# Spreading the sample states over more ticks and reordering a norm's pilot, extra columns and row tokens

## The chip, the cores and the metric

One NeuronCore of a Trainium2 chip runs the whole program. The metric is the device time of one execution in microseconds (us); of several runs the median is given. The engines are named as in the profile: PE (TensorE, matmuls), DVE (VectorE), ACT (ScalarE), POOL (GpSimd) and SP (SyncE, which here only issues DMAs). Each engine works through its instructions in the order written; where one waits, all behind it on that engine wait too.

## The reference

One layer of a hybrid decoder is computed for 256 prompt tokens and 8 sample tokens (T = 264 columns), width 2048, in float32:

- `proj = x @ w_in`, cut into z, x/B/C, dt, the short convolution's three parts and two gates;
- A: a Mamba-2 SSD mixer (32 heads of 64, 4 groups, state 128) with a causal convolution before it. For the prompt it is a chunked scan. Each of the 8 samples takes one step on a state of its own: `h = h * exp(dt*A) + (x*dt) B`, `y = h C`; the new states (8 x 2048 x 128) are outputs;
- B: a gated short convolution; `mix = sigmoid(g_a) * (yA @ w_branch_ssd) + sigmoid(g_b) * (yB @ w_branch_sc)`;
- `x1 = LN(ALPHA*x + mix @ w_out)`, then `x2 = LN(ALPHA*x1 + PEER(x1))`, where PEER picks 16 of 16384 single-neuron experts for each of 8 heads, and last `y = x2 + sigmoid(x2 @ ple_gate_w) * (p @ ple_proj_w)`.

## The kernel before

**Weights and matmuls.** Activations lie transposed: 128 rows of the width by the tokens. Weights come in 1 MB tiles `w` (16 blocks of 128 x 128) that SP fetches in a written-out order (`fetch`, L146) into a ring of three. `split_w` cuts each half tile in two: `whi`, a rounded copy made by ACT (L158), and `wlo`, the remainder made by DVE (L159), into four pairs of buffers, later five. `col_block` computes 128 output rows in two halves, each of 8 x 3 matmuls (L255 whi by x high, L256 whi by x low, L257 wlo by x high). `pair_block` does the same for the experts' matrices with two matmuls a block (L293, L294, L296).

**Ticks.** After each half block `tick` is called. It first runs what `defer` and `soon` have put by for this tick, then lets the background tasks, which are Python generators, go on in the order of their list. A number that a task yields is taken from the tick's credit (0.9 to 1.3, an estimate of VectorE's time), and `("w", n)` lets the task rest for n ticks. All of this is fixed when the program is built: it sets only the order of the instructions on each engine. `soon` is the next tick, or the one after it where it is called from an evacuation.

**Sample states.** `ssd_samples` goes over 64 units of 256 state rows. An iteration issues, for units of different age: the store of the new state (POOL, L659), the read-out `jk` (two on DVE, L665), the update (two on DVE, L675), the scaling by the decay (two on ACT, L681), and the loads of a state tile `h0t` (SP, L692; a ring of eight) and of B and C (SP, L696; every second unit). It runs beside the x/B/C blocks (24 column blocks, with a convolution evacuated by `conv_evac`), the short convolution's blocks (48, `sc_c`, `sc_h`, `sc_b`), and `ssd_group`, the prompt's scan (four groups; ACT loads `arow`, L557). SP's queue holds the weight fetches and the state loads in one order. Ahead of the z stage `run_out` gives ticks with no matmul until scan and samples are done.

**Norms.** `Norm` takes 16 blocks as they are evacuated (`add`). The first block gives a pilot mean (`pilot`: PE L876, ACT L878), which is subtracted from all (`gather`, DVE L886). For each block j the scaled block is written as a high part `h` (ACT, L894) and a low part `l` (DVE, L910), squares are taken (ACT, L895), sums kept (DVE, L912 or L915), and two extra columns of gain and bias are put into `h` and `l` (POOL, L896, L897); the next matmul reads all of it. In the second norm the 208 prompt columns come from the V product (`v_evac`: L1480, L1482), and the other 56 columns, the row tokens, whose experts are gathered row by row on POOL, come later from `rest`: for each j a high part (ACT, L948), a copy (POOL, L949) and a low part (DVE, L952). The PLE product (`ple_half`, L1559 to L1561) comes behind the last block of V, then the norm's statistics, then the last 16 column blocks.

Of the kernel before, what the change touches and what calls it, by code (L numbers as in the profile page):

```python
# [20 lines left out]
T = PT + NS  # L21
# [30 lines left out]
def hybrid_step(ctx: ExitStack, tc: tile.TileContext, xT, pT, w_in, w_dt, w_bs, w_bc, w_o, w_q, w_pg, w_pp,  # L52
# [590 lines left out]
    def ssd_samples():  # L643

        while len(XS) < 4 or "dexp" not in S or "bc" not in S:
            yield ("w", 1)
        dexp = S["dexp"]
        xds, hts, bcs = {}, {}, {}
        units = [(g, s, a) for g in range(GRP) for s in range(NS) for a in range(2)]
        n = len(units)  # L650

        def rows(t, u):
            g, s, a = units[u]
            return t[s, 512 * g + 256 * a:512 * g + 256 * a + 256, :].rearrange("(q p) n -> p q n", p=128)

        u = 0
        while u < n + 4:
            if 0 <= u - 4:
                gp.dma_start(out=rows(o_hs, u - 4), in_=hts.pop(u - 4))  # L659
            if 0 <= u - 3 < n:  # L660
                v = u - 3
                g, s, a = units[v]
                for q in range(2):
                    jk = ab("jk", width=128)
                    ve.scalar_tensor_tensor(jk, hts[v][:, q], 1.0, bcs[v // 2][:, 1], OP.mult, OP.mult,  # L665
                                            accum_out=ysum[:, 4 * g + 2 * a + q, s:s + 1])
                if (s, a) == (NS - 1, 1):
                    for q in range(4):
                        j = 4 * g + q
                        ve.scalar_tensor_tensor(XS[j][:, PT:], XS[j][:, PT:], col(P_D, j), ysum[:, j], OP.mult, OP.add)  # L670
            if 0 <= u - 2 < n:
                v = u - 2
                g, s, a = units[v]
                for q in range(2):
                    ve.scalar_tensor_tensor(hts[v][:, q], bcs[v // 2][:, 0], xds[g][:, 2 * a + q, s:s + 1],  # L675
                                            hts[v][:, q], OP.mult, OP.add)
            if 0 <= u - 1 < n:
                v = u - 1
                g, s, a = units[v]
                for q in range(2):  # L680
                    ac.activation(hts[v][:, q], hts[v][:, q], AF.Copy, scale=dexp[:, 4 * g + 2 * a + q, 1, s:s + 1])  # L681
            if u < n:
                g, s, a = units[u]
                while 4 * g + 3 not in XS:
                    yield ("w", 1)
                if (s, a) == (0, 0):
                    xd = ep.tile([128, 4, NS], F, name="xd", tag="xd", bufs=2)
                    for q in range(4):
                        ve.tensor_tensor(xd[:, q], XS[4 * g + q][:, PT:], dexp[:, 4 * g + q, 0], OP.mult)
                    xds[g] = xd  # L690
                h = ep.tile([128, 2, 128], F, name="h0t", tag="h0t", bufs=8)
                sy.dma_start(out=h, in_=rows(h0, u))  # L692
                hts[u] = h
                if a == 0:
                    b = ab("bcb", width=256)
                    sy.dma_start(out=b, in_=bass.AP(tensor=bc_d.tensor, offset=bc_d.offset + (u // 2) * 256,  # L696
                                                    ap=[[0, 128], [1, 256]]))
                    bcs[u // 2] = b.rearrange("p (a n) -> p a n", a=2)
            u += 1
            yield 0.45  # L700
            yield ("w", 1)

    def ssd_all():
        for g in range(GRP):
# [151 lines left out]
    class Norm:  # L856
        def __init__(self, g_base, b_base, name, new, w=T):
            self.g, self.b, self.name, self.new = g_base, b_base, name, new
            self.w = w
            self.h, self.l = [], []  # L860
            self.gb = []
            src = cpar[:, g_base:g_base + 32].rearrange("p (a j) -> p j a", a=2)
            h = cpool.tile([128, 16, 2], R, name=name + "gbh")
            l = cpool.tile([128, 16, 2], R, name=name + "gbl")
            ac.copy(h, src)
            ve.tensor_tensor(l, src, h.bitcast(F), OP.subtract)
            self.gb = [h.bitcast(F), l.bitcast(F)]
            self.s0 = None
            self.c = None
            self.d = []  # L870
            self.n = 0
            self.acc = None

        def pilot(self):
            ps = bank("pil")
            te.matmul(ps[:, :self.w], o128, self.s0[:, :self.w], start=True, stop=True)  # L876
            self.c = block("pc")
            ac.copy(self.c[:, :self.w], ps[:, :self.w])  # L878
            self.gather(self.s0)

        def gather(self, s):

            j = len(self.d)
            w = self.w
            beside = w < T
            ve.tensor_tensor(s[:, :w], s[:, :w], self.c[:, :w], OP.subtract)  # L886
            self.d.append(s[:, :T])
            h, l = self.new(self.name)
            hv, lv = halves(h)[:, :, :w // 2], halves(l)[:, :, :w // 2]
            sv = even_odd(s[:, :w])  # L890
            q = s[:, w:2 * w] if beside else block("dsq")

            def on_act():
                ac.activation(hv, sv, AF.Copy, scale=col(self.g, j))  # L894
                ac.activation(q, s[:, :w], AF.Square)  # L895
                gp.tensor_copy(halves(h)[:, :, T // 2], self.gb[0][:, j])  # L896
                gp.tensor_copy(halves(l)[:, :, T // 2], self.gb[1][:, j])  # L897
                if j == 0:
                    if beside:
                        a = lp.tile([128, 2, w], F, name="da", tag="as", bufs=2)  # L900
                        gp.tensor_copy(a.rearrange("p a t -> p (a t)"), s)
                        self.acc = [(a[:, 0], a[:, 1])]
                        self.both = a.rearrange("p a t -> p (a t)")
                    else:
                        a = block("da")
                        gp.tensor_copy(a, s)
                        self.acc = [(a, q)]

            def on_dve():
                ve.scalar_tensor_tensor(lv, sv, col(self.g, j), hv.bitcast(F), OP.mult, OP.subtract)  # L910
                if j and beside:
                    ve.tensor_tensor(self.both, self.both, s, OP.add)  # L912
                elif j:
                    for a, x in zip(self.acc[0], (s, q)):
                        ve.tensor_tensor(a, a, x, OP.add)  # L915
                self.n += 1

            self.h.append(h)
            self.l.append(l)
            soon(on_act)  # L920
            soon(on_dve)

        def rest(self, xs, sq):

            w, n = self.w, T - self.w
            yield ("w", 2)
            ps = bank("pil")
            te.matmul(ps[:, :n], o128, xs[:, 0], start=True, stop=True)
            c = block("pc")[:, :n]
            ac.copy(c, ps[:, :n])  # L930
            yield ("w", 1)
            ve.tensor_tensor(xs, xs, c[:, None, :].to_broadcast([128, 16, n]), OP.subtract)
            yield 1.0
            yield ("w", 1)
            a = block("da")[:, 0:2 * n].rearrange("p (a t) -> p a t", a=2)
            ac.activation(sq, xs, AF.Square)
            ve.tensor_reduce(a[:, 0], xs.rearrange("p j t -> p t j"), AX.X, OP.add)
            yield 1.0
            yield ("w", 1)
            ve.tensor_reduce(a[:, 1], sq.rearrange("p j t -> p t j"), AX.X, OP.add)  # L940
            self.acc.append((a[:, 0], a[:, 1]))
            yield 1.0
            for j in range(16):
                while self.n <= j:
                    yield ("w", 1)
                h, l = (halves(v[j])[:, :, w // 2:T // 2] for v in (self.h, self.l))
                x = even_odd(xs[:, j])
                ac.activation(h, x, AF.Copy, scale=col(self.g, j))  # L948
                gp.tensor_copy(self.d[j][:, w:], xs[:, j])  # L949

                def low(h=h, l=l, x=x, j=j):
                    ve.scalar_tensor_tensor(l, x, col(self.g, j), h.bitcast(F), OP.mult, OP.subtract)  # L952

                soon(low)
                yield 0.2

        def add(self, s):
            if self.s0 is None:
                self.s0 = s
                soon(self.pilot)  # L960
            else:
                self.gather(s)

# [732 lines left out]
```

## Time and profile before

| | us |
|---|---|
| median of 3 runs | 2480.94 |
| lowest and highest | 2480.01 and 2483.31 |
| the profiled execution's own time | 2488.03 |
| its span in the profile | 2486.3 |

The profile is of one execution. It gives for each engine its busy time and, for each instruction, how long the engine had been idle before it and which instruction ended that wait. A tile's name stands for all its buffers, and `L692` is line 692 of the kernel. "SPq" and "POOLq" are queues that issue DMAs. Matmuls overlap in PE, so the busy time of PE says less than the number of matmuls in a stretch of time.

### The profile page before, as it was taken

To read this page: it belongs to the slowest core of one execution; us is meant where nothing else is said; L and a number is where in the kernel's file an instruction comes from. 1 tells how busy PE (TensorE), PEld (TensorE's weight loads), DVE (VectorE), ACT (ScalarE), POOL (GpSimd) and SP (SyncE) were. 2 spreads that over 40 slices of the span, in tenths; PEclk is the share of its full clock that TensorE was granted. 3 is DMA by queue.
4 is the path that set the end of the run, shared out by engine and by line. 5 is a ranking of instruction groups with operands and counts; after the bars stand their busy time and mean duration, and the time that the engine had idled before them with its cause. 6 is when DMAs were issued, how large, how long until landed. Compare 5 with 4: busy or idle time off the path is not lost.

```text
span 2486.3 us, 47938 instructions
## 1 busy us (share of the span) xinstructions
PE 2427.8 (98%) x19049; PEld 2399.4 (97%) x19049; DVE 2008.8 (81%) x3192; ACT 1459.5 (59%) x2310; POOL 606.5 (24%) x720
## 2 busy tenths in 40 slices
PE   9999999999999999999999999999999999999989
PEld 9999999999999999998999999999999999999989
DVE  8889865567455578999998778769899999899987
ACT  6776654455444455754777788866544555445564
POOL 2332200000000010100345666632332323323201
PEclk9999999999999999999999999999999999999999
DMA  6788755555555555566779999999999999999554
GB/s 250 250 293 277 256 190 189 199 194 189 201 188 202 190 201 187 195 211 202 243 290 341 357 360 371 370 348 399 394 371 381 383 378 395 364 372 379 200 176 148
DMA packets 137105, 688.91 MB, mean 277 GB/s; under 512 B 15744, under 2 KB 53168, under 8 KB 63280
## 3 DMA queue, kind: packets, MB, share of 16 engines
q1 hardware_dynamic: 89168, 495.46, 55.9%
q0 software_dynamic: 28688, 158.69, 16.5%
q10 hardware_dynamic: 19024, 31.69, 3.5%
q8 instruction: 149, 2.44, 0.4%
q14 instruction: 76, 0.62, 0.1%
HBM read 646.32 MB, written 39.46 MB: 276 GB/s over the span
## 4 chain that ended last, share of the span: by engine, by line
PE 57%; DMA 15%; DVE 15%; issue 6%; ACT 6%; POOL 1%; ACTq 0%; SPq 0%; DVEq 0%; POOLq 0%
PE mm L255 12%; PE mm L257 12%; PE mm L256 12%; PE mm L293 10%; DVE wlo L159 7%; DMA w<-vP 6%; PE mm L294 5%; DMA w<-uT 4%; ACT whi L158 3%; DMA h0t<-h 2%; DVE ug L1363 1%; ACT o L1270 1%; DVE acc L1480 1%; DMA o_hs<-h0t 1%; DMA ug<-vR,sidx 1%
## 5 line engine op out<-in xcount | busy, mean ns | idle before, releaser
L159 DVE TENSOR_TENSOR wlo<-w,whi 128x1024 fp32r<-128x1024 f32 x916 | 1112.3, 1222 | 359.7 <-ACT whi L158 354.1
L158 ACT CAST whi<-w 128x1024 fp32r<-128x1024 f32 x916 | 943.8, 1044 | 611.8 <-DMA w<-vP 249.8
L293 PE MATMUL mm<-x,whi 128*128 128x416 f32 x1920 | 572.8, 365 | 4.1 <-ACT whi L158 4.1
L293 PE MATMUL mm<-co,whi 128*128 128x416 f32 x1920 | 562.1, 361 | 0.0
L255 PE MATMUL mm<-x,whi 128*128 128x264 f32 x1920 | 533.9, 278 | 4.4 <-ACT whi L158 4.4
L257 PE MATMUL mm<-x,wlo 128*128 128x264 f32 x1920 | 532.2, 277 | 5.2 <-DVE wlo L159 5.0
L256 PE MATMUL mm<-x,whi 128*128 128x264 f32 x1920 | 531.1, 277 | 0.0
L294 PE MATMUL mm<-x,wlo 128*128 128x208 f32 x2048 | 505.1, 257 | 16.0 <-DVE wlo L159 15.7
L294 PE MATMUL mm<-co,wlo 128*128 128x208 f32 x2048 | 501.2, 255 | 8.4 <-DVE wlo L159 8.1
L294 PEld LDWEIGHTS mm<-x,wlo 128*128 128x128 f32 x2048 | 392.7, 193 | 26.3 <-DVE wlo L159 25.5
L294 PEld LDWEIGHTS mm<-co,wlo 128*128 128x128 f32 x2048 | 390.6, 192 | 13.8 <-DVE wlo L159 13.7
L257 PEld LDWEIGHTS mm<-x,wlo 128*128 128x128 f32 x1920 | 363.9, 190 | 7.2 <-DVE wlo L159 7.2
L293 PEld LDWEIGHTS mm<-x,whi 128*128 128x128 f32 x1920 | 365.5, 190 | 5.6 <-ACT whi L158 4.4
L255 PEld LDWEIGHTS mm<-x,whi 128*128 128x128 f32 x1920 | 364.2, 190 | 6.2 <-ACT whi L158 4.8
L256 PEld LDWEIGHTS mm<-x,whi 128*128 128x128 f32 x1920 | 364.1, 190 | 0.0
L293 PEld LDWEIGHTS mm<-co,whi 128*128 128x128 f32 x1920 | 363.3, 189 | 0.0
L1269 POOL TENSOR_SCALAR o<-iot,slot,slot 128x128 f32<-128x128 f32 x156 | 184.4, 1188 | 2.7 <-issue 0.9
L1293 POOL DMA_INDIRECT ug<-vR,sidx x56 | 105.5, 1885 | 270.6 <-DVE x1s L1373 227.2
L1293 POOL DMA_INDIRECT ug<-uR,sidx x56 | 92.1, 1644 | 274.3 <-DVE ug L1363 198.2
L1363 DVE SCALAR_TENSOR_TENSOR ug<-ug,x1s 128x2048 f32<-128x2048 f32 x56 | 127.7, 2281 | 2.1 <-DMA ug<-uR,sidx 2.1
L1373 DVE SCALAR_TENSOR_TENSOR x1s<-ug,scf,x1s 128x2048 f32<-128x2048 f32 x53 | 124.1, 2342 | 0.0
L896 POOL CAST r1h<-r1gbh 128x2 fp32r<-128x2 f32 x16 | 7.0, 438 | 439.9 <-DVE mxl L242 439.9
(364 smaller groups left out, 3936.6 us busy)
## 6 DMA issues: line engine op xcount, KB each, us to landing
w<-uT SPq DMA_DIRECT2D x128, 1024.0 KB, 7.2
w<-vP SPq DMA_DIRECT2D x128, 1024.0 KB, 8.9
w<-w_in SPq DMA_DIRECT2D x118, 1024.0 KB, 4.9
w<-w_bc SPq DMA_DIRECT2D x16, 1024.0 KB, 4.9
w<-w_bs SPq DMA_DIRECT2D x16, 1024.0 KB, 4.9
w<-w_o SPq DMA_DIRECT2D x16, 1024.0 KB, 4.9
w<-w_q SPq DMA_DIRECT2D x16, 1024.0 KB, 4.9
w<-w_pg SPq DMA_DIRECT2D x16, 1024.0 KB, 5.0
```

What stands on the lines that cost most here:

```text
L158: ac.copy(hi, w)
L159: ve.tensor_tensor(lo, w, hi.bitcast(F), OP.subtract)
L255: te.matmul(ps, wh, vh, start=(first and q == 0), stop=False)
L256: te.matmul(ps, wh, vl, start=False, stop=False)
L257: te.matmul(ps, wl, vh, start=False, stop=(last and q == n - 1))
L293: te.matmul(ps, hi[:, ws], both, start=(kb == 0), stop=False)
L294: te.matmul(ps[:, :TD], lo[:, ws], one, start=False, stop=False)
L1269: (gp if q < 3 else ve).tensor_scalar(o1[:, q], iot, slot[0][:, c], slot[2][:, c], OP.is_equal, OP.mult)
L1270: ac.activation(o2[:, q], iot, AF.Abs, bias=slot[1][:, c], scale=-1.0)
L1293: gp.indirect_dma_start(out=t, out_offset=None, in_=tab, in_offset=bass.IndirectOffsetOnAxis(ap=sidx[:, c:c + 1], axis=0))
L1363: ve.scalar_tensor_tensor(t, t, 1.0, x1s, OP.mult, OP.mult, accum_out=shid[:, c:c + 1])
L1373: ve.scalar_tensor_tensor(x1s, t, scf[:, c:c + 1], x1s, OP.mult, OP.add)
```

## The change

In `ssd_samples` the rest after each iteration alternates between two ticks and one; the scaling of a unit comes two iterations after its load instead of one, and update, read-out and store each come one iteration later than they did. In `Norm` the pilot runs four ticks after the first block instead of at the next chance, and the blocks that have come by then are gathered together; the two extra columns are written at once in `gather` instead of behind ACT's part a tick later; and `rest` takes block j only when block j + 2 has been summed.

```
-        while u < n + 4:
-            if 0 <= u - 4:
-                gp.dma_start(out=rows(o_hs, u - 4), in_=hts.pop(u - 4))
-            if 0 <= u - 3 < n:
-                v = u - 3
+        while u < n + 5:
+            if 0 <= u - 5:
+                gp.dma_start(out=rows(o_hs, u - 5), in_=hts.pop(u - 5))
+            if 0 <= u - 4 < n:
+                v = u - 4
...
-            if 0 <= u - 2 < n:
-                v = u - 2
+            if 0 <= u - 3 < n:
+                v = u - 3
...
-            if 0 <= u - 1 < n:
-                v = u - 1
+            if 0 <= u - 2 < n:
+                v = u - 2
...
             u += 1
             yield 0.45
-            yield ("w", 1)
+            yield ("w", 1 + u % 2)
...
+            self.first = []
 
         def pilot(self):
...
-            self.gather(self.s0)
+            for s in self.first:
+                self.gather(s)
...
             sv = even_odd(s[:, :w])
+            gp.tensor_copy(halves(h)[:, :, T // 2], self.gb[0][:, j])
+            gp.tensor_copy(halves(l)[:, :, T // 2], self.gb[1][:, j])
             q = s[:, w:2 * w] if beside else block("dsq")
 
             def on_act():
                 ac.activation(hv, sv, AF.Copy, scale=col(self.g, j))
                 ac.activation(q, s[:, :w], AF.Square)
-                gp.tensor_copy(halves(h)[:, :, T // 2], self.gb[0][:, j])
-                gp.tensor_copy(halves(l)[:, :, T // 2], self.gb[1][:, j])
...
             for j in range(16):
-                while self.n <= j:
+                while self.n <= min(j + 2, 15):
                     yield ("w", 1)
...
             if self.s0 is None:
                 self.s0 = s
-                soon(self.pilot)
+                defer(4, self.pilot)
+            if self.c is None:
+                self.first.append(s)
             else:
                 self.gather(s)
```

## The prediction

> **What bounds the kernel now.** I read the page first, then the waits of TensorE, then tables of stages, and only then single instructions. The page says that TensorE (PE) is all but full:
>
> ```profile
> PE 2427.8 (98%) x19049; PEld 2399.4 (97%) x19049; DVE 2008.8 (81%) x3192; ACT 1459.5 (59%) x2310; POOL 606.5 (24%) x720
> ```
>
> So only the places where PE stands still can pay. The waits of PE (total, times, longest) name them:
>
> ```profile
> PE mm L1559 <- DVE acc L1480: 7.2, 2, 4.9
> PE mm L257 <- DVE wlo L159: 5.0, 8, 0.8
> PE mm L255 <- ACT whi L158: 4.4, 2, 3.4
> PE pil L876 <- DVE acc L1482: 2.0, 1, 2.0
> ```
>
> L255 and L257 are column blocks, the stage of the sample states; L1559 and L876 are the end of the V product and the second norm. A wait is not the whole loss, since PE also runs slower after it; matmuls per stage show that. In these rows the number in brackets counts instructions; PE, PEld, DVE, ACT, POOL come in this order, then the granted clock and the share of the DMA engines.
>
> ```profile
> 100.00:150.00 50.00, 49.94 (x444) 49.74 (x444) 49.36 (x154) 39.83 (x96) 22.36 (x45) 1.00 0.89 295
> 150.00:200.00 50.00, 43.84 (x353) 42.55 (x352) 41.03 (x131) 35.75 (x78) 12.77 (x25) 0.93 0.83 278
> 200.00:250.00 50.00, 50.00 (x455) 48.93 (x454) 45.88 (x144) 30.94 (x67) 14.25 (x26) 1.00 0.89 289
> 250.00:300.00 50.00, 47.58 (x427) 45.92 (x426) 46.21 (x144) 33.04 (x68) 15.06 (x26) 1.00 0.82 265
> 300.00:350.00 50.00, 50.00 (x455) 48.93 (x454) 33.30 (x48) 28.82 (x53) 3.82 (x11) 1.00 0.57 192
> ```
>
> A full stage with SSD groups in it issues 455. The second row lacks 102 and the fourth 28: 130 matmuls at 50/455 = 0.11 us are **14.3 us**, twice what the waits on whi and wlo say. The fifth row is the same work without samples: VectorE (DVE) falls from 92% to 67%, DMA from 0.82 to 0.57.
>
> **The sample states (L692 load, L681 scale on ACT, L675 update and L665 read-out on DVE, L659 store).** Removed and added: nothing; 64 units are spread from one a tick (a tick is half a column block) to two in three ticks, the scaling comes two iterations after its load instead of one, the later steps move along by one.
>
> ```profile
> 127.60 0.50 DVE jk L665 x4
> 128.11 0.53 DVE h0t L675 x2
> ...
> L665 DVE SCALAR_TENSOR_TENSOR jk<-h0t,bcb x128: 275/284/342, 96.8 to 298.6; 128x128 f32<-128x128 f32 x128
> ```
>
> One unit costs DVE 0.50 + 0.53 = 1.03 us (the chain of waits). 64 units took 201.8 us by the read-outs; less the 14.3 lost that is 187.5/64 = 2.93 us a tick. At a unit a tick samples take 1.03/2.93 = 35% of DVE; on top of the 67% of the fifth row that is 102%: DVE is over-full, and whatever lead it has over PE is eaten (99% in the first row). At two units in three ticks they take 23%, so 90%; the first row goes from 99% to 87%. In a stretch of 64 ticks a third of the units, 22 us of DVE work, moves behind 300 us, where a third of DVE is free. That exceeds the 14.3.
>
> How the loss comes about is seen in ACT and SP at the first SSD group:
>
> ```profile
> 165.41 0.53 ACT L746 ACTIVATE cacc<-pad,cpar 128x288 f32<-128x288 f32 x1 [4.19 <-DVE pad L744]
> ...
> 176.49 0.69 ACT L681 ACTIVATE h0t<-h0t,dexp 128x128 f32<-128x128 f32 x2 [3.79 <-DMA h0t<-h]
> ```
> ```profile
> 159.39 7.47 SPq L692 DMA_DIRECT2D h0t<-h  x2
> ```
> ```profile
> DMA to landing us min/median/max: 2.2/5.2/9.6
> ```
>
> ACT waits 4.19 us for a late DVE, then 3.79 us for a state whose load SP got out late (two issues took 7.47 us). The next weights' whi stand behind L681 on ACT, wlo behind them on DVE. A load was asked one tick (2.9 us) before its use, less than the median landing of 5.2; now it is 3 ticks, 8.8 us, which covers the median and, with the old 3.79 as the worst lack, that case too. Both causes go. What stays late next is ACT's own burst at each group; I leave 2 us for it and take **12 us** of gain. Ends: 14.3, all of it, and below zero, since a state tile now lives six iterations instead of five in a ring of eight. SP, behind which every weight fetch stands, already waits for that ring:
>
> ```profile
> SPq L692 <- DMA o_hs<-h0t: 13.1, 15, 2.2
> ```
>
> Counted in ticks a tile's next load comes 4.5 after its store instead of 4, so this should shrink; were it to double and reach PE, it would cost 13. I take the value near the upper end because the 13.1 us passed without one PE wait on a DMA. POOL only issues the stores later.
>
> **The second norm.** Its blocks run at DVE's pace (L1480 is each block's evacuation):
>
> ```profile
> 2322.18 0.58 DVE L1480 TENSOR_TENSOR acc<-mm,acc 128x416 f32<-128x416 f32 x1
> ...
> 2326.91 0.58 DVE L1480 TENSOR_TENSOR acc<-mm,acc 128x416 f32<-128x416 f32 x1
> ...
> 2365.24 0.43 DVE L910 SCALAR_TENSOR_TENSOR r<-acc,cpar,r 128x208 fp32r<-128x208 f32 x1 [0.20 <-POOL r L897]
> ...
> 2367.03 1.22 DVE L159 TENSOR_TENSOR wlo<-w,whi 128x1024 fp32r<-128x1024 f32 x1 [0.84 <-ACT whi L158]
> 2368.17 0.58 DVE L1480 TENSOR_TENSOR acc<-mm,acc 128x416 f32<-128x416 f32 x1
> ...
> 2374.02 0.58 DVE L1480 TENSOR_TENSOR acc<-mm,acc 128x416 f32<-128x416 f32 x1
> ```
>
> 4.73 us a block while only the prompt columns are done, 5.85 in the last blocks, where the row tokens' parts run in step. DVE's idle time there, and who makes it:
>
> ```profile
> DVE wlo L159 <- ACT whi L158: 5.8, 7, 1.7
> ...
> DVE r L910 <- POOL r L897: 2.6, 10, 0.8
> ```
> ```profile
> POOL r L896 <- ACT r L894: 60.1, 16, 5.6
> ...
> POOL acc L949 <- DVE da L912: 7.0, 5, 2.8
> ```
> ```profile
> ACT r L894 <- DVE acc L886: 29.7, 14, 4.2
> ...
> ACT r L948 <- DVE r L910: 6.7, 5, 2.5
> ```
> ```profile
> 2365.71 0.35 ACT L948 ACTIVATE r<-x1sp,cpar 128x56 fp32r<-128x56 f32 x1 [1.20 <-DVE r L910]
> ```
>
> The loop of the last blocks: L886, ACT L894, POOL L896 and L897, DVE L910, ACT L948, whi, wlo. The extra columns first: POOL's two copies come off it, L910's wait goes; nine of the ten, at 0.20, lie before the last evacuation: 1.8 us. The parts two blocks on: L948 and L949 ask for an L910 and L912 long done, so ACT starts whi 1.20 earlier and the 0.84 of DVE goes, in three blocks before the last evacuation: 2.5 us. Two L952 (0.27 by the row below) fall behind that evacuation: 0.5 us. Sum **4.8 us**, on PE's path because PE waits 4.9 us for the last L1480. What moves to the end (three L948, L949, L952 in a burst) is covered by the PLE matmuls:
>
> ```profile
> L952 DVE SCALAR_TENSOR_TENSOR r<-x1sp,cpar,r x16: 264/269/271, 2353.8 to 2386.3; 128x56 fp32r<-128x56 f32 x16
> ```
>
> Without that cover it would be 0.5 us. Ends: 0, if DVE finds another wait, and 4.8 plus the slow stretch after the PE wait:
>
> ```profile
> 2380.00:2390.00 10.00, 9.49 (x59) 9.49 (x59) 6.10 (x10) 6.32 (x16) 0.54 (x3) 0.69 0.57 188
> 2390.00:2400.00 10.00, 10.00 (x89) 10.00 (x89) 6.14 (x9) 7.00 (x13) 0.00 (x0) 1.00 0.36 129
> ```
>
> 30 matmuls fewer at a clock of 0.69 are 3.4 us, so 8.2. I don't count it: PE waits from the last evacuation but one to the last, that gap falls from 5.85 to 5.0, and the wait from 4.9 to 4.1. The 3.4 us at L255 lie in the stage with a clock of 0.93, so 4.1 should slow it too. The Trainium skill (TensorE: Matmul & The Clock Gate, "What's actually happening") says that the clock halves after an idle window of about 3.4 us; the row agrees that it fell after 4.9, and by the rule 4.1 would still do it, so its sum is mine.
>
> **The pilot four ticks later.** PE no longer stands 2.0 us at L876. But DVE sets this stage's end, and it lost at most one wait for whi there, so I put it at zero (0 to 2.0). The first gathers come as a pair, the same work; their L896 stand on POOL behind the last indirect gathers, which the later pilot lets pass. In the first norm no wait of PE is listed: nothing, all hidden by PE.
>
> **Sum.** 12 + 4.8 = 16.8 us off the profiled execution's 2488.03 (span 2486.3 and 1.7 around it): 2471.2. The runs' median, 2480.94, lies 7.1 below that execution; the same difference gives **2464.1**.
>
> **Rivals.**
> 1. *Only the samples pay*: DVE, freed of two waits, finds another in the last blocks. For it: ACT waits 29.7 us on L886 anyway. 2480.9 - 12 = 2469.
> 2. *The burst at the first SSD group remains*: 102 of the 130 lost matmuls lie in one window, and the arow loads and ACT's tables stay. Then only the 28 (3.1 us) and the 4.8 go: 2473. Against it: DVE at 87% arrives there with its lead.
> 3. *POOL ahead of ACT turns into a wait of ACT*. L894 now has to follow L896, and that copy is often stretched:
>
> ```profile
> L896 POOL CAST r<-r2gbh x16: 186/594/2067, 2297.9 to 2383.1; 128x2 fp32r<-128x2 f32 x16
> ```
>
> If it starts no earlier, the loop keeps the copy, the 1.8 stays, and the median 0.59 in three blocks takes 1.8 back: 2467.7. Against it: POOL need not wait for L886, on which ACT spent 29.7 us. The Trainium skill (SBUF — State Buffer, "Who interferes with whom") has the reason for such copies: GpSimd reads are blocked whole by a VectorE instruction with two SBUF inputs. The spread from 186 to 2067 agrees.
> 4. *The sample stream runs out of ticks* (slower). It has 69 iterations, 103.5 ticks from about tick 25, and the column blocks ahead of the z stage end at tick 144 (72 blocks of two). What is left then runs with no matmul beside it. It decides from some 21 missed ticks on (16 of margin; 5.7 more at 2.93 us eat the gain of 16.8). If every second iteration waited one tick more, that would be 34, so 18 past the end, each between DVE's 1.03 and a whole tick's 2.93 us: 19 to 53 us on top, 2483 to 2517, in the middle 2500. Against it: samples are first in the list and claim 0.45 of a tick's credit of 0.9 to 1.3. The margin in time:
>
> ```profile
> L782 ACT ACTIVATE sz<-mm x16: 390/390/392, 459.1 to 540.1; 128x264 f32<-128x264 f32 x16
> ```
>
> read-outs begin at 96.8 and would end 64 x 1.5 x 2.93 = 281 us later, at 378.
> 5. *Nothing moves*: SP's ring takes the place of ACT's wait, and the gains are given back: 2481.
>
> **How the numbers follow.** Forecast 0.54; rivals 1: 0.13, 2: 0.12, 3: 0.05, 4: 0.06, 5: 0.10. A measurement can tell about 0.2%, 5 us, from no change. Faster takes forecast and 1 to 3: 0.84; same 0.10; slower 0.06. Low: 2480.9 - 14.3 - 8.2 = 2458; high: rival 2 with twice the 2 us left for the burst, 2477. Outside lie 4, 5 and the edges.
>
> **What would show it.** Right: 450 or more matmuls in each 50 us from 150 to 300; read-outs until about 378; no wait of ACT on h0t near 4 us; DVE near 90%. L896 before L894; no L910 wait on POOL; last blocks near 5.0 us; the PE wait at L876 gone. Wrong: SP waiting on o_hs beyond 13 us, PE still short at the first SSD group, or L910 late for another reason.

## The result and the profile after

The changed kernel takes **2464.46 us** (median of 6 runs, 2459.17 to 2466.22), the kernel before, run beside it, 2481.48 (6 runs, 2476.11 to 2483.31): a ratio of **0.9923, interval 0.9909 to 0.9936**, or 17.0 us. Two more sets of runs of the changed kernel gave 0.9915 [0.99, 0.9929] and 0.9917 [0.9901, 0.9934]. The profiled execution after took 2465.26 us with a span of 2463.5, which is 22.8 less than the profiled execution before. Cut at three instructions, that difference is:

| stretch of the span, us | before | after | less |
|---|---|---|---|
| start to the first `sz` of the z stage (L782) | 459.1 | 445.2 | 13.9 |
| from there to the first evacuation of the last expert chunk (L1480, now L1484) | 1835.4 | 1832.7 | 2.7 |
| first to last evacuation of that chunk | 85.38 | 80.01 | 5.4 |
| from there to the end | 106.4 | 105.6 | 0.9 |

The second row holds the first norm, which has the edits too, but the profiles show no gain there: in the fourteen of this study it lies between 1828.5 and 1835.4, with the norms' edits and without them, so its 2.7 is scatter. The first and third row are the change. The third would be larger without one accident of this execution, shown below: the four other profiles with all three of the norms' edits have 78.1 to 78.3 there.

The waits of PE after (total, times, longest):

```profile
PE mm L294 <- DVE wlo L159: 23.1, 31, 2.8
PE mm L1563 <- DVE acc L1484: 4.8, 2, 3.7
PE mm L293 <- ACT whi L158: 4.1, 2, 3.5
```

The column blocks and the pilot are gone from the top of the list, and the wait for the last evacuation (L1563, which was L1559) fell from 7.2 to 4.8 in all, the longest from 4.9 to 3.7. L293 and L294 are the experts, which the change does not touch.

The sample stages after, in the same columns as before (PE, PEld, DVE, ACT, POOL with counts, granted clock, DMA share):

```profile
100.00:150.00 50.00, 50.00 (x447) 50.00 (x446) 46.04 (x115) 40.40 (x93) 18.54 (x40) 1.00 0.81 266
150.00:200.00 50.00, 50.00 (x450) 49.31 (x448) 43.98 (x125) 37.26 (x76) 13.49 (x26) 1.00 0.85 285
200.00:250.00 50.00, 50.00 (x447) 49.14 (x446) 42.62 (x118) 34.49 (x72) 11.15 (x19) 1.00 0.78 255
250.00:300.00 50.00, 50.00 (x461) 49.41 (x460) 41.31 (x109) 32.08 (x64) 10.55 (x19) 1.00 0.81 268
300.00:350.00 50.00, 50.00 (x455) 48.93 (x454) 42.19 (x120) 31.09 (x64) 12.59 (x21) 1.00 0.83 273
```

PE has 447 to 461 matmuls in every 50 us and its clock is 1.00 throughout, where it had 353 and 427 with a clock of 0.93 in the worse stage. DVE works 83 to 92% of each instead of 82 to 99% of the first four and 67% of the fifth: the samples' work now lies over all of them.

```profile
L665 DVE SCALAR_TENSOR_TENSOR jk<-h0t,bcb x128: 278/284/332, 104.1 to 391.8; 128x128 f32<-128x128 f32 x128
```

The read-outs end at 391.8 and not at 298.6.

The end of the second norm, on DVE (start, duration, instruction):

```profile
2348.68 0.58 DVE L1484 TENSOR_TENSOR acc<-mm,acc 128x416 f32<-128x416 f32 x1
2349.29 0.38 DVE L1486 TENSOR_TENSOR acc<-acc 128x208 f32<-128x208 f32 x1
2349.70 0.38 DVE L888 TENSOR_TENSOR acc<-acc,pc 128x208 f32<-128x208 f32 x1
2349.99 0.27 DVE L954 SCALAR_TENSOR_TENSOR r<-x1sp,cpar,r 128x56 fp32r<-128x56 f32 x1
2350.18 1.22 DVE L159 TENSOR_TENSOR wlo<-w,whi 128x1024 fp32r<-128x1024 f32 x1
2351.32 0.43 DVE L912 SCALAR_TENSOR_TENSOR r<-acc,cpar,r 128x208 fp32r<-128x208 f32 x1
2351.66 0.59 DVE L914 TENSOR_TENSOR da<-da,acc 128x416 f32<-128x416 f32 x1
2352.17 1.22 DVE L159 TENSOR_TENSOR wlo<-w,whi 128x1024 fp32r<-128x1024 f32 x1
2353.30 0.58 DVE L1484 TENSOR_TENSOR acc<-mm,acc 128x416 f32<-128x416 f32 x1
```

These are all of DVE's instructions there. From one evacuation to the next are 4.62 us, where the last blocks had 5.85, and no row carries a wait: neither L912 (the L910 of before) for POOL, nor `wlo` for `whi`. The row tokens' low part (L954, once L952) adds the 0.19 from its start to that of the next `wlo`; without it a block is 4.44, as the middle blocks now are (4.73 before).

The waits between 2270 and 2365:

```profile
ACT r L898 <- DVE acc L888: 24.7, 11, 4.1
...
ACT r L898 <- POOL r L893: 3.4, 2, 3.0
...
DVE wlo L159 <- ACT whi L158: 2.7, 2, 1.8
DVE r L912 <- ACT r L898: 0.5, 1, 0.5
```

The second row looks like POOL's extra columns (L893) holding up the high part (L898) by 3.0 us. But L898 also reads what DVE's subtraction (L888) writes, and in the trace that one ended at 2296.15 and L893 at 2296.19: POOL came last by 0.04 us. It cost DVE nothing; the 0.5 us of the last row lie behind the last evacuation, at 2361.16. The 1.8 us of the third row are the accident: behind the first of the 16 evacuations a weight tile landed late.

```profile
2279.73 2.00 ACT L158 CAST whi<-w 128x1024 fp32r<-128x1024 f32 x2 [5.05 <-DMA w<-vP]
```

DVE waited 1.82 us for this `whi`, and the next evacuation came after 5.17 us instead of the 3.3 of the four other profiles. The 10 us that begin with the last evacuation, before, after, and in two of the runs below (`s_only`, where the norms are as before, and `all_again`, the changed kernel once more):

```profile
2379.87:2389.87 10.00, 9.36 (x58) 9.36 (x58) 6.23 (x11) 6.32 (x17) 0.54 (x3) 0.68 0.56 182
2357.93:2367.93 10.00, 9.36 (x67) 9.36 (x68) 6.90 (x14) 7.63 (x22) 0.40 (x2) 0.83 0.55 193
2363.37:2373.37 10.00, 9.36 (x66) 9.31 (x67) 6.40 (x12) 7.17 (x20) 0.54 (x3) 0.82 0.55 184
2353.11:2363.11 10.00, 9.37 (x55) 9.37 (x56) 6.60 (x13) 6.42 (x18) 0.39 (x2) 0.66 0.55 194
```

The wait of PE that ends 0.6 us into each of them is 4.9, 3.7, 4.9 and 3.7 us long, the matmuls are 58, 67, 66 and 55: the slow stretch varies from execution to execution and does not follow the wait.

### The profile page after: what moved, and what is told of

Its sections match the earlier page's. It is cut to its first block, busy times and chain, and to the rows that moved or that the text cites. A ratio compares the mean times of both kernels' runs of the same rounds, so it can differ in the third digit from the quotient of the medians.

```text
span 2463.5 us, 47946 instructions
## 1 busy us (share of the span) xinstructions
PE 2418.6 (98%) x19049; PEld 2394.8 (97%) x19049; DVE 2008.5 (82%) x3192; ACT 1458.7 (59%) x2310; POOL 620.0 (25%) x720
## 4 chain that ended last, share of the span: by engine, by line
PE 63%; DVE 15%; DMA 11%; ACT 5%; issue 5%; ACTq 0%; POOL 0%; DVEq 0%; SPq 0%; POOLq 0%
PE mm L255 14%; PE mm L257 14%; PE mm L256 14%; PE mm L293 11%; DVE wlo L159 7%; PE mm L294 6%; DMA w<-vP 5%; DMA w<-uT 4%; ACT whi L158 2%; DVE ug L1367 1%; PE gps L1286 1%; ACT o L1274 1%; PE mm L296 1%; DMA a_d<-as 1%; DMA g_d<-gs 1%
## 5 line engine op out<-in xcount | busy, mean ns | idle before, releaser
L293 PE MATMUL mm<-x,whi 128*128 128x416 f32 x1920 | 572.7, 365 | 4.1 <-ACT whi L158 4.1
L293 PE MATMUL mm<-co,whi 128*128 128x416 f32 x1920 | 561.8, 361 | 0.0
L294 PE MATMUL mm<-x,wlo 128*128 128x208 f32 x2048 | 504.7, 257 | 16.2 <-DVE wlo L159 15.9
L294 PE MATMUL mm<-co,wlo 128*128 128x208 f32 x2048 | 500.8, 255 | 7.2 <-DVE wlo L159 7.2
L294 PEld LDWEIGHTS mm<-x,wlo 128*128 128x128 f32 x2048 | 392.8, 193 | 25.0 <-DVE wlo L159 24.4
L294 PEld LDWEIGHTS mm<-co,wlo 128*128 128x128 f32 x2048 | 390.7, 192 | 11.5 <-DVE wlo L159 11.4
L293 PEld LDWEIGHTS mm<-x,whi 128*128 128x128 f32 x1920 | 365.6, 190 | 5.8 <-ACT whi L158 4.6
L293 PEld LDWEIGHTS mm<-co,whi 128*128 128x128 f32 x1920 | 363.3, 189 | 0.0
L1273 POOL TENSOR_SCALAR o<-iot,slot,slot 128x128 f32<-128x128 f32 x156 | 191.1, 1232 | 2.7 <-issue 0.9
L893 POOL CAST r1h<-r1gbh 128x2 fp32r<-128x2 f32 x16 | 7.5, 468 | 439.9 <-DVE mxl L242 439.9
```

The lines of the kernel that those rows point to most:

```text
L293: te.matmul(ps, hi[:, ws], both, start=(kb == 0), stop=False)
L294: te.matmul(ps[:, :TD], lo[:, ws], one, start=False, stop=False)
L1273: (gp if q < 3 else ve).tensor_scalar(o1[:, q], iot, slot[0][:, c], slot[2][:, c], OP.is_equal, OP.mult)
```

## The experiments

The theory: the sample states cost PE time because they overfill DVE for 64 ticks, and spreading them pays by that alone; in the second norm, POOL's copies and the row tokens' parts each add DVE waits of their own. The rivals: the samples pay because a state is asked for earlier (**latency**), and the norm's edits pay only together, or only because PE no longer waits at the pilot. "z" below is the start of the first `sz`, "evacuations" the time from the first to the last evacuation of the last expert chunk (85.38 before). All ratios are to the kernel before on the same chip.

**Samples' part alone, and the norms' part alone.**

> The samples' part of the change whole (two units in three ticks, scaling two iterations after the load), the norms as before. Theory (two separate terms that add up): the stage of the samples loses nothing more, 13.9 us come off ahead of the z stage as in the changed kernel's profile (first sz at 445.2 instead of 459.1), the median falls by 10 to 14 us; the second norm keeps its 2.0 us PE wait at the pilot and 4.9 us at the PLE product. Rival (only the samples pay, the norm's edits merely shift a wait): the whole 17 us of the medians come from here.

2468.63 us against 2485.41, ratio 0.9924 [0.991, 0.9937]; z at 445.6, evacuations 85.47. The medians fall by 16.8 us, more than the theory's 10 to 14 and about the 17 of the rival; by this run's time alone the rival could stand.

> The norms' part of the change whole, the samples as before. Theory: from the first evacuation of the last expert chunk to the last one 5.3 us less than before, as in the changed kernel's profile, nothing ahead of it; the median falls by 4 to 7 us. Rival (the norm's edits only pay beside the samples', or not at all): within 2 us of before.

2476.51, ratio 0.9958 [0.9945, 0.9971]; z at 462.5, evacuations 78.11. The interval excludes no change, so the norms' edits pay by themselves: 8.9 us of the medians, where 4 to 7 were expected, and 7.3 us of evacuations instead of 5.3. Each part moves its own stretch. z is 3.4 us later than before although nothing ahead of it was edited, so at a unit a tick z itself varies by some 3 us between executions.

**The cadence alone, and the earlier loads alone.**

```
             yield 0.45
-            yield ("w", 1)
+            yield ("w", 1 + u % 2)        # s_cadence: only this
```

> Only the pace of the samples, two units in three ticks; the scaling still one iteration after its load. Theory of the load (VectorE over-full at a unit a tick): PE loses less than 3 us between 100 and 300, first sz within 3 us of 445, 10 to 14 us off the median, although a load now has only 1.5 ticks on average. Rival of the latency (the state is asked too late): ACT still waits about 4 us for h0t at the first SSD group, PE loses 8 us or more there, the median falls by 5 us at most.

2470.79, ratio 0.9931 [0.9918, 0.9945]; z at 445.7. Its two worst stages of before:

```profile
100.00:150.00 50.00, 50.00 (x447) 50.00 (x446) 46.32 (x119) 40.40 (x93) 20.96 (x41) 1.00 0.83 268
150.00:200.00 50.00, 49.82 (x445) 49.02 (x445) 43.43 (x120) 36.77 (x75) 12.89 (x26) 1.00 0.84 281
```

For s_ahead the scaling, update, read-out and store come one iteration later, as in the change, at a unit a tick:

```
-            yield ("w", 1 + u % 2)
+            yield ("w", 1)                # the rest of the samples' part stays
```

> Only the two iterations between load and scaling, still a unit a tick. Theory of the load: VectorE stays above 90% from 100 to 300, PE loses 8 us or more, the median falls by 5 us at most; SP waits longer for the ring of eight than the 13.1 us of before, since a tile's next load comes three ticks after its store instead of four. Rival of the latency: ACT's wait for h0t goes and with it the loss at the first SSD group, PE loses less than 4 us, 9 us or more off the median.

2484.43, ratio 1.0 [0.9988, 1.0011]; z at 459.2.

```profile
100.00:150.00 50.00, 47.68 (x419) 47.09 (x419) 46.43 (x145) 39.05 (x94) 23.66 (x44) 1.00 0.80 261
150.00:200.00 50.00, 44.50 (x375) 42.54 (x374) 42.97 (x137) 36.78 (x79) 15.39 (x26) 1.00 0.91 289
```

DVE works 93 and 86% of these two stages, where the theory had above 90 throughout. SP's queue of that kernel, among the fetches of weights (L146):

```profile
SPq L692 <- DMA o_hs<-h0t: 87.3, 27, 7.4
```

The cadence gives the whole of the samples' gain, the earlier loads give none. They do shorten ACT's worst wait for a state from 3.8 to 1.2 us, but at a unit a tick the six iterations that a state now lives meet the ring of eight: SP's wait for a store to leave its tile grows from 13.1 to 87.3 us, and all weight fetches stand behind it. ACT's `whi` then waits 14.1 us for weights between 100 and 350 us, where the list of before has no such row. So this run does not price the late state by itself, since what it takes away there may be lost again on the weights; a longer ring at a unit a tick was not run. The cadence also ends every listed wait of ACT for a state between 100 and 350 us. What speaks against latency as the cause is the order of events before, read below: between 137 and 155 us the split had next to no lead left, and ACT's first wait for a state ends at 176.5.

**Two more doses of the cadence.** Instead of `1 + u % 2`:

```
+            yield ("w", 1 + u % 4 // 3)        # s_quarter: 1.25 ticks a unit
+            yield ("w", 1 + min(u % 4, 1))     # s_threeq: 1.75 ticks a unit
```

> Samples at one and a quarter ticks a unit, nothing else changed. A third dose between one tick (z stage begins at 459.1) and one and a half (445.7). Load theory: VectorE's sum is 67 + 35/1.25 = 95%, still under 100, so most of the loss goes: z stage from 446 to 450, read-outs until about 340, time 0.993 to 0.996 of before. If it were the distance from load to use that counts (3.7 us here, 2.9 before, 4.4 at one and a half, a landing median of 5 us), half would go at most: 452 or later. If the gain is in proportion to the ticks added, half: 452.

2473.87 against 2485.06, ratio 0.9954 [0.9937, 0.997]; z at 451.5, read-outs until 342.2.

```profile
100.00:150.00 50.00, 50.00 (x447) 50.00 (x446) 48.71 (x143) 41.38 (x96) 24.58 (x44) 1.00 0.87 282
150.00:200.00 50.00, 46.61 (x395) 44.77 (x394) 40.58 (x114) 35.33 (x71) 13.00 (x23) 1.00 0.84 275
```

> Samples at one and three quarter ticks a unit, nothing else changed. VectorE's sum is 67 + 35/1.75 = 87%, which pays no more than 90% did: z stage at 445.5 as with one and a half. 68 iterations are 119 ticks from about tick 25, so 144, where the column blocks end: the prediction's fourth rival begins here. If no tick is missed, z begins at 445.5 and the time is 0.993 of before; each missed tick past the end costs 1.03 to 2.93 us, so five missed would be 450 to 460 and eat the gain.

2467.84, ratio 0.9932 [0.9914, 0.995]; z at 445.6, read-outs until 432.2. The four doses give z at 459.1, 451.5, 445.7 and 445.6: somewhat over half the gain at 1.25 and nothing more beyond 1.5. With z varying by some 3 us, 451.5 does not tell the theory's 450 from the 452 of "half". But at 95% of DVE a good part of the loss is still there, so the threshold just below 100% is too simple.

What is missing at 1.25 can be read from the traces as a lead: the time from the end of a `wlo` on DVE to the first matmul that reads it. One half block before, and the same one at 1.25 ticks:

```profile
144.45 1.22 DVE L159 TENSOR_TENSOR wlo<-w,whi 128x1024 fp32r<-128x1024 f32 x1
145.72 0.38 PE L257 MATMUL mm<-x,wlo 128*128 128x264 f32 x1
```
```profile
141.42 1.22 DVE L159 TENSOR_TENSOR wlo<-w,whi 128x1024 fp32r<-128x1024 f32 x1
145.86 0.28 PE L257 MATMUL mm<-x,wlo 128*128 128x264 f32 x1
```

A lead of 0.05 us stands against one of 3.2. In the seven half blocks that PE begins between 137 and 155 us the lead is 0.1 to 1.6 us before, 2.7 to 4.2 at 1.25 and 3.3 to 6.0 at 1.5. So at 1.25 DVE, busy for 97% of the stage, does enter the first SSD group with a lead, and the group uses it up: from 177.6 to 188.6 us four half blocks in a row have 0.1 us. At 1.5 the lead falls to 0.1 us in one half block, at 184.9. A coarser sign stands in the list of waits between 100 and 350 us, before:

```profile
ACT cacc L746 <- DVE pad L744: 35.7, 10, 6.6
DVE wlo L159 <- ACT whi L158: 23.8, 16, 4.9
ACT h0t L681 <- DMA h0t<-h: 6.7, 3, 3.8
ACT whi L158 <- PE mm L256: 5.8, 5, 1.4
```

and with the cadence alone:

```profile
ACT cacc L746 <- DVE pad L744: 27.6, 11, 4.0
ACT whi L158 <- PE mm L256: 20.0, 11, 2.6
DVE wlo L159 <- ACT whi L158: 15.9, 20, 1.5
```

`whi` waiting for PE means that the split is so far ahead that all its buffers are full: 5.8 us of that before, 3.7 at 1.25 ticks, 20.0 at 1.5. The row doesn't grow step by step with the gain; it shows a full lead, not a partial one. ACT's waits for the convolution's `pad` shrink only to 27.6; with the lead PE waits 0.2 us in all between 100 and 350 us, where it waited 8.5.

With 1.75 ticks the fourth rival, ticks running out, was to begin. The read-outs end 13 us ahead of z and nothing is lost. A larger dose was not tried, so the loss itself was not seen.

**The norm's three edits one by one**, each on top of the samples' part (2468.63 and evacuations of 85.47 without them).

```
             sv = even_odd(s[:, :w])
+            gp.tensor_copy(halves(h)[:, :, T // 2], self.gb[0][:, j])   # n_cols: only these two moved
+            gp.tensor_copy(halves(l)[:, :, T // 2], self.gb[1][:, j])
...
+                while self.n <= min(j + 2, 15):                         # n_rest: only this
...
+                defer(4, self.pilot)                                    # n_pilot: only this, with self.first
```

> On top of the samples' part, only the extra columns first; pilot and row tokens' parts as before. From the first to the last evacuation of the last expert chunk it is 85.4 us in four kernels without the norms' edits and 80.0 with all three. Theory of the prediction (each edit takes away its own wait): L910's 0.20 us on POOL goes in nine blocks, 1.8 us, so 83.6; the four last blocks still take 5.6 us or more, since ACT's row part still waits for L910. Rival (POOL ahead of ACT becomes a wait of ACT): 85 or more. Time: within 0.2% of the samples' part alone.

2468.17 (ratio 0.9941 [0.9923, 0.9958]); evacuations 82.29, so 3.2 less. Middle blocks 4.44 instead of 4.73, last blocks 5.56 instead of 5.85. That is 0.29 a block for a listed wait of 0.20:

```profile
2307.33 1.22 DVE L159 TENSOR_TENSOR wlo<-w,whi 128x1024 fp32r<-128x1024 f32 x1
2308.46 0.43 DVE L910 SCALAR_TENSOR_TENSOR r<-acc,cpar,r 128x208 fp32r<-128x208 f32 x1
```

Without a wait L910 begins 0.08 us before the `wlo` ahead of it has ended; the list counts idle time from that end, and so leaves out this overlap.

> On top of the samples' part, only the row tokens' parts two blocks on. Theory of the prediction: ACT's 1.20 us wait for L910 and VectorE's 0.84 us wait for whi go in three blocks, and two L952 fall behind the last evacuation: 3.0 us, so 82.4 us, the last blocks at 5.0 and the earlier ones still at 4.73. Rival (the two edits only work together, since POOL's copies stand behind its row copies, which still come after ACT): last blocks stay above 5.5, 84 or more. Time: 0 to 5 us less than the samples' part alone.

2469.01 (0.9935 [0.9922, 0.9948]); evacuations 82.27, 3.2 less: middle blocks 4.73 as before, last blocks 4.91.

> On top of the samples' part, only the pilot four ticks later and the first blocks gathered together. Theory: PE's wait at the pilot (1.3 to 2.0 us) goes, but VectorE sets this stage's end: 85.4 us plus or minus 1, time within 3 us of the samples' part alone. Rival (the pilot's stall is passed on by PE to the end): 83.5 or less, 2 us off the time.

2467.93 (0.993 [0.9917, 0.9943]); evacuations 84.48, 1.0 less, all of it in the first three blocks; PE's wait for the pilot is gone, and the other blocks stay at 4.73 and 5.86.

> The changed kernel once more, beside the parts. Theory (terms add up): 80.0 us for the 16 evacuations, and 4 to 7 us less time than the samples' part alone, 0.988 to 0.991 of before. Rival (the norms' edits pay only where the samples' stall shifts the stages): no faster than the samples' part alone, 0.992 to 0.993 of before.

2462.63 (0.9915 [0.99, 0.9929]); evacuations 78.09. The waits of PE:

```profile
PE mm L294 <- DVE wlo L159: 19.2, 31, 2.8
PE mm L1563 <- DVE acc L1484: 4.7, 2, 3.7
```

3.2 + 3.2 + 1.0 = 7.4 is what all three together give, 85.47 - 78.09 = 7.4: the terms add, and none needs another. In time the three are too small to be told apart (their intervals overlap). Together they show: this run lies 5.3 to 6.4 us below the three single edits, which ran beside it, though its 0.9915 is just outside the 0.988 to 0.991 of the theory.

**The change without the earlier loads**, and the change itself beside it.

> The changed kernel without the state loads asked two ahead: cadence and all three norm edits. If asking two ahead gives nothing on top of the cadence: same as the changed kernel in this call within 3 us (0.991 to 0.993 of before), z stage at 445.7, evacuations of the last expert chunk in 78 us. If it saves or costs something in the executions that the profile does not show, they differ by 4 us or more.

2463.45, ratio 0.9919 [0.9902, 0.9935]; z at 445.5, evacuations 78.29.

> The changed kernel again, beside the three others on the same chip: 0.9915 to 0.993 of before, z stage at 445.2, evacuations of the last expert chunk in 78 to 80 us. What differs from the profile of the first call of it is scatter between executions.

2462.72, ratio 0.9917 [0.9901, 0.9934]; z at 445.1, evacuations 78.11. It and the run without the earlier loads lie 5.1 and 4.4 us below the one at 1.75 ticks, which ran beside them without the norms' edits.

Three of the change's five edits (cadence, columns, row parts) carry its gain, the pilot a little, and the moved loads neither help nor harm. No version here beats the changed kernel by more than the runs can tell.

## Why the prediction was right, and where its steps were not

The forecast of 2464.1 met 2464.46, closer than its terms deserve; that part is luck, as the sum at the end shows. Its terms by those of the profile:

- **Samples, 12 forecast, 13.9 measured.** All of the 14.3 lost came back but 0.4; the 2 us left for ACT's burst were not needed. DVE's sum was right in kind: 102% loses, 90% does not (92, 88, 85, 83 and 84% measured). As a threshold it was too simple, since 95% at 1.25 ticks still lost about half; an SSD group uses up a lead of 2.7 to 4.2 us there. (The 14.3 are 1.5 times the 9.4 us of the waits on `whi` and `wlo`, not twice.)
- **The cause named for it was wrong in one step.** I wrote that the two waits of ACT, 4.19 for `pad` and 3.79 for a late state, were how the loss comes about and that both go. The wait for `pad` stayed (4.0 at the longest with the cadence) and hardly reached PE any more. The one for the state, taken down to 1.2 by the earlier loads alone, gave nothing back, in a run in which the weights came late. Both were on the way to the PE wait of 3.4 us, but the lead of `wlo` was down to 1.6 us or less from 137 us on, ahead of both. What the late state would cost by itself stays open.
- **SP's ring "should shrink": it did not.** It was 13.1 and is 14.2 in the profile after and 18.2 in another of the same kernel; this was one of the signs of being wrong, and harmless, as I took it to be. At the old cadence it is 87.3. Counting ticks from a store to the next load left out how long the store waits on POOL for the update on DVE: 45.0 us in all before (3.1 at the longest), 57.0 after (5.4).
- **Two signs of being right were missed by a little.** One 50 us stage has 447 matmuls, not 450. The read-outs end at 391.8, not 378: they begin at 104.1 instead of 96.8, since a read-out now comes four iterations of 1.5 ticks behind its load instead of three of one, and a tick took 3.0 us.
- **Extra columns, 1.8 forecast, 3.2 measured.** I took nine waits of 0.20. Nine blocks became 0.26 to 0.29 shorter, which is the wait and the overlap of 0.08. Four more became 0.11 to 0.19 shorter; in three of them L910 had begun 0.08 us after the end of the `wlo` before it, which the list does not count as a wait.
- **Row parts, 3.0 forecast (2.5 and 0.5), 3.2 measured.** The last blocks were to be 5.0 and are 4.91 with this edit alone (the wait of 0.84 and the overlap again); with all three 4.62, which is DVE's own work.
- **The pilot, 0 forecast (0 to 2.0), 1.0 measured.**
- **The slow stretch behind the last evacuation.** I counted none of it, arguing that a wait of 4.1 us would still slow PE. The wait became 3.7, and PE was still slowed. (My row did not show that the clock fell after 4.9 us: in the trace of before it is at half from 3.9 us ahead of the last evacuation on, which is 0.4 us into that wait, and in the run at 1.25 ticks it falls at the end of the wait of 2.3 us that comes before the last one.) What I left out is how much the stretch varies: the 10 us from the last evacuation on ran at 0.83 in one profile of the changed kernel and at 0.66 in another, against 0.68 before and 0.82 in `s_only`. From the last evacuation to the end it is 105.6 to 107.1 us in the five profiles with all the norms' edits and 105.2 to 106.6 in the six with none, so no gain can be booked for it.
- **Rivals.** The third, POOL ahead of ACT becoming a wait of ACT, did not come about: the wait of 3.0 us in the list has POOL last by 0.04. The first, second and fifth are excluded by the evacuations at 78 to 80, by 450 matmuls in the stage of the first group, and by the ratios; the fourth by the read-outs, which end 53 us ahead of z.

**The sum and the median.** The terms seen in the profiles are 13.9 and 5.4 to 7.4, so 19 to 21, where I had 16.8. The median moved 17.0 in the first set of runs, and by the ratios 0.9915 and 0.9917 about 21 in the others; the intervals of the three overlap. I carried the 7.1 us by which the profiled execution stood above its median over to the changed kernel, whose profiled execution stood 0.8 above. Part of that difference is the stretch of 1835.4 in the table above, one of the two longest that were seen. The forecast was so close because terms that were 2 to 4 too small met a set of runs in which the gain came out some 4 smaller than in the two later ones. That stretch differs by 7 us between executions, and PE's waits at L293 and L294 in it, which add to 19 to 28 us, go with it: over the fourteen profiles it is 0.87 us longer for each us of these waits (correlation 0.89). Why the split is later there in one execution than in another stays open.

## What to carry to other kernels

Where background work shares an in-order engine that feeds TensorE, measure the lead and not only the wait: the time from the end of a piece to the first instruction that reads it, ahead of a burst and within it. Here a lead of 0.1 to 1.6 us ahead of the first burst went with a loss of 14.3 us, one of 2.7 to 4.2 with about half of that, and one of 3.3 to 6.0 with next to none. Asking for data earlier lengthens the life of its buffer; beside a ring of eight it moved the wait from the engine to the queue that issues the loads. In a stage that DVE paced, a listed wait was a lower bound of what its cause cost, by the 0.08 us that the next instruction would have overlapped: set the time from one block to the next against the sum of the engine's own work in it.

## What the runs showed of the hardware

Most spacings of the evacuations repeat to 0.1 us from one kernel and execution to the next (the fifth is 4.73 to 4.75 in every kernel without the norm's edits and 4.43 to 4.44 in every one with all of them, the last three 5.85 to 5.87 and 4.62 to 4.64), while a stretch of 1830 us in which no edit shows varies by 6.9. So an edit of 1 us can be read in its own stage of one profile, though medians of six runs do not show it. One late weight tile can still hide it: the first spacing is 5.17 in one profile of the changed kernel and 3.26 to 3.28 in two others.

POOL's copies of two elements a partition are as irregular after the change as before:

```profile
L893 POOL CAST r<-r2gbh x16: 176/207/1194, 2278.8 to 2348.8; 128x2 fp32r<-128x2 f32 x16
L894 POOL CAST r<-r2gbl x16: 176/184/2317, 2279.0 to 2348.9; 128x2 fp32r<-128x2 f32 x16
```

The longest of them took as long as the instruction with two inputs that DVE ran beside it:

```profile
2296.07 2.35 DVE L1377 SCALAR_TENSOR_TENSOR x1s<-ug,scf,x1s 128x2048 f32<-128x2048 f32 x1
2296.13 2.32 POOL L894 CAST r<-r2gbl 128x2 fp32r<-128x2 f32 x1
```

The first L894 of this norm took 1.18 us in `all_again`, beside a `wlo` of DVE, and 0.18 in the profile after, where DVE stood idle:

```profile
2276.08 1.18 POOL L894 CAST r<-r2gbl 128x2 fp32r<-128x2 f32 x1
```
```profile
2278.99 0.18 POOL L894 CAST r<-r2gbl 128x2 fp32r<-128x2 f32 x1
```

The Trainium skill (SBUF — State Buffer, "Who interferes with whom") gives such DVE instructions as a reason for this spread; these rows, 0.18 us without one and 1.18 and 2.32 beside one, agree.
